# Root mean squares of a four-layer encoder on one core: the sum matmul spreads its result over all partitions, the root and reciprocal are taken on 256 columns, and fewer products are made ahead

## The chip, the core and the metric

The kernel runs on one core of a Trainium2 chip. The metric is device time in microseconds (us) of one execution of the whole program, in which all weights are read from HBM once. All data are float32. TensorE (PE in the profile) multiplies, VectorE (DVE) and ScalarE (ACT) work element by element, GpSimd (POOL) makes a few masks, and SyncE (SP) issues the loads of the weights.

## The reference

The input is 256 positions of 1024 features. Four layers each do a half-step feed-forward block, a mixer and another half-step feed-forward block; every block is normed before and after.

```python
def rms_norm(x, g):
    y = x * lax.rsqrt(jnp.mean(x * x, axis=-1, keepdims=True) + EPS)
    return y * g

def swiglu(h, w_in, w_out):
    gate, up = jnp.split(h @ w_in, 2, axis=-1)          # 1024 -> 2 x 2816
    return (jax.nn.silu(gate) * up) @ w_out             # 2816 -> 1024

for i in range(4):
    x = x + 0.5 * rms_norm(swiglu(rms_norm(x, g[0]), ff1_in[i], ff1_out[i]), g[1])
    h = rms_norm(x, g[2])
    m = mixer(i % 3)(h)         # 0: chunked attention, 1: gMLP, 2: differential attention
    x = x + rms_norm(m, g[3])
    x = x + 0.5 * rms_norm(swiglu(rms_norm(x, g[4]), ff2_in[i], ff2_out[i]), g[5])
```

So there are 12 blocks (8 feed-forward blocks, 4 mixers), 12 norms ahead of a block and 12 behind one. Each norm needs, for each of the 256 positions, one sum of squares over 1024 features, a root and a reciprocal.

## The kernel before

**Layout.** Features lie on the partitions, positions on the columns: the residual `xr` is 128 partitions x 8 tiles x 256 columns. A sum over features is therefore a sum over 8 tiles (done on DVE, tile by tile) and then over 128 partitions (done by a matmul).

**Products.** Each float32 factor is split into a high part (ACT, lines 127 and 315) and a low remainder (DVE, lines 130 and 330), both of a type that PE multiplies quickly; a product is made of three matmuls (high x high, low x high, high x low). Weights come in pieces of 128 x 1024 through three raw buffers; the class `Stream` splits them some pieces ahead of their use. The order of work on PE, DVE and ACT is the order in which the program writes it down.

**The end of a block.** `Branch.tile_done` (line 369) is called for each of the 8 output tiles: ACT squares the tile (line 376) and scales it by the gain (line 377), DVE adds the square to a running sum (line 387). At the last tile the sum over partitions is taken in two steps, once for the running sum and once for the last square: `column_sums` (line 237) uses the squares as the stationary operand and one column of ones as the moving one, in two halves of 128 positions, so that the sums come out with positions on the partitions (128 x 2). `Branch.finish` (line 393) takes the root (ACT, line 247) and the reciprocal (DVE, line 249) of these 128 x 2 numbers. Then `spread2` turns them back into a row that stands on all partitions: two matmuls (line 254) with the column repeated 128 times as the stationary operand and the identity as the moving one. DVE reads this row from PSUM (`fb`).

**The start of the next block.** `Normed` works in the order of `PARTS`: tiles 6, 7, 4 and 5, 0 and 1, 2 and 3. For each part DVE multiplies the tile by `fb` (line 476) and adds it to the residual (line 482), ACT takes the high part (line 315), DVE the low part (line 330). The first products of the next block follow in the same order of tiles (`JOIN`): four column blocks of weights, lines 510 (narrow) or 694 (wide). The norm ahead of the block is applied only later, to the products: `sums` and `spread` of `Normed` make its row `bc` from the sum of squares in the same way (`column_sums`, root, reciprocal on 128 x 2, `spread2`), and ACT copies it to SBUF (line 345). The three attention blocks use both the 128 x 2 form (`tok`) and the row; the gMLP block sends `tok` through DRAM (`spread_later`).

**Products made ahead.** Between the last product of one block and the first of the next PE would have nothing to do. `Ahead` fills this with products of the next block for some feature tiles `ks`. Since the update is x + y·f with f not yet known, it makes the products of x and of y separately (into two PSUM tiles, `ps` and `share`) for the first of the four column blocks; `scale` multiplies the y part by f later (line 458 or 461 and 462) and `join` adds the two (line 466). In `project_pair` and `Wide.block` the products that were made ahead are left out. There are two forms:

- narrow (weights stationary, 256 columns, line 451): from a mixer to the second feed-forward block (4 times, with `late=True`, where the y parts are made as `YLATE` says) and from a feed-forward block to the next layer (3 times). `ks` is (0, 1, 2, 3, 5): 5 tiles x 3 matmuls x 2 (x and y) = 30 matmuls ahead, 15 left out later.
- wide (activations stationary, 512 columns, line 449): from the first feed-forward block to the mixer, 4 times. `ks` is (1, 2, 3): 18 matmuls ahead, 9 left out later. Here only the first half of the positions is made ahead, and f is used as a 128 x 1 column (`update.f[:, 0:1]`, line 458).

The matmuls ahead are handed out in portions: 4 between the two sums (each wide one counts as two), 8 while the root is taken, the rest behind `spread2`. At the very end of the program there is no next block, and matmuls on a constant (`Warm`, line 233) stand in their places.

Of the kernel before, what the change touches and what calls it, by code (L numbers as in the profile page):

```python
# [9 lines left out]
F32 = mybir.dt.float32  # L10
BF16 = mybir.dt.bfloat16
F32R = mybir.dt.float32r
AF = mybir.ActivationFunctionType
# [3 lines left out]
P = 128  # L17
D = 1024
S = 256
# [28 lines left out]
ORDER = _order(range(KD))  # L48

PARTS = ((6, 7), (7, 8), (4, 6), (0, 2), (2, 4))  # L50
YLATE = {4: (0, 1, 2), 5: (3, 5)}
JOIN = _order([k for a, b in PARTS for k in range(a, b)])
DUMMY = [2, 1, 1] + [1, 0, 0] * 3 + [0] * 12

# [2 lines left out]
def encoder_trunk_kernel(  # L57
# [14 lines left out]
    nc = tc.nc  # L72

    const = ctx.enter_context(tc.tile_pool(name="const", bufs=1))
    wpool = ctx.enter_context(tc.tile_pool(name="wpool", bufs=3))
    act = ctx.enter_context(tc.tile_pool(name="act", bufs=1))
    tmp = ctx.enter_context(tc.tile_pool(name="tmp", bufs=2))
# [9 lines left out]
    class Stream:  # L87


        def __init__(self):  # L90
            self.pieces = {}
            self.raws = []
            self.now = 0
            self.split_next = 0
            self.allowed = SLOTS
            self.held = True
            self.pending = None
# [89 lines left out]
    def bank():  # L187
        return pst.tile([P, 512], F32, tag="pst", name="pst_t")
# [24 lines left out]
    nc.scalar.preload_act_table(AF.Sqrt)  # L213
    ident = const.tile([P, P], F32, name="ident")
    make_identity(nc, ident)
    ones = const.tile([P, 2], F32, name="ones")
    nc.vector.memset(ones, 1.0)
    eps_t = const.tile([P, 1], F32, name="eps_t")
    nc.vector.memset(eps_t, EPS)
    eps2_t = const.tile([P, 1], F32, name="eps2_t")  # L220
# [13 lines left out]

    Warm()(WARM)

    def column_sums(ps, sq, first, last):
        for h in range(2):
            nc.tensor.matmul(  # L239
                ps[:, h:h + 1], sq[:, h * P:(h + 1) * P], ones[:, 0:1],  # L240
                start=(first and h == 0), stop=(last and h == 1), skip_group_check=True,
            )

    def inv_sqrt(src, bias, n, scale):

        sd = small.tile([P, n], F32, tag=f"sd{n}", name="sd")
        nc.scalar.activation(sd, src, AF.Sqrt, bias=bias, scale=scale)
        r = small.tile([P, n], F32, tag=f"rs{n}", name="rs")
        nc.vector.reciprocal(r, sd)
        return r  # L250

    def spread(col, ps):

        nc.tensor.matmul(ps, col.broadcast_to([P, P]), ident, start=True, stop=True)  # L254

    def spread2(r):
        ps = bank()
        for h in range(2):
            spread(r[:, h:h + 1], ps[:, h * P:(h + 1) * P])
        return ps[:, 0:S]  # L260

    class Normed:

# [68 lines left out]
                    op0=ALU.mult, op1=ALU.subtract,  # L332
                )

        def sums(self, func):
            ps = bank()
            column_sums(ps, self.acc[:, 0, :], True, True)
            self.tok = inv_sqrt(ps[:, 0:2], eps_t, 2, 1.0 / D)
            nc.scalar.preload_act_table(func)

        def spread(self):

            ps = spread2(self.tok)
            self.bc = tmp.tile([P, S], F32, tag="rbc", name="rbc", bufs=1)
            nc.scalar.copy(self.bc, ps)

        def spread_later(self):

# [5 lines left out]
    class Branch:  # L354
# [15 lines left out]
        def tile_done(self, d, ps):  # L370
            if d == 0:
                self.acc = tmp.tile([P, S], F32, tag="ysq", name="ysq", bufs=1)
                if not self.yg:
                    self.yg = act.tile([P, KD, S], F32, tag="yg", name="yg")
            sq = tmp.tile([P, S], F32, tag="sq1", name="sq1") if d > 0 else self.acc
            nc.scalar.activation(sq, ps, AF.Square)
            nc.scalar.activation(self.yg[:, d, :], ps, AF.Copy, scale=self.gain[:, d:d + 1])
            if d == KD - 1:
                self.ss = bank()
                column_sums(self.ss, self.acc, True, False)  # L380
                self.fill = self.ahead or Warm()
                if self.ahead:
                    self.ahead.begin()
                self.fill(4)
                column_sums(self.ss, sq, False, True)
            elif d > 0:
                nc.vector.tensor_tensor(self.acc, self.acc, sq, op=ALU.add)
            elif self.n:
                nc.vector.scalar_tensor_tensor(self.acc, self.n.acc[:, 0, :], EPS, sq, op0=ALU.mult, op1=ALU.add)
            if self.ahead:  # L390
                self.ahead.tile_done(d, self.yg)

        def finish(self):

            f = inv_sqrt(self.ss[:, 0:2], eps2_t if self.n else eps_t, 2, 1.0 / D)
            self.fill(8)
            fb = spread2(f)
            self.fill(36 if self.ahead else 12)
            return Update(self.yg, f, fb, self.ahead)

    class Ahead:


        def __init__(self, gain, wide=False, late=False):
            self.gain, self.wide, self.late = gain, wide, late
            self.ks = (1, 2, 3) if wide else (0, 1, 2, 3, 5)
            self.x, self.y, self.todo = {}, {}, []

        def parts(self, dst, src, scale):
# [44 lines left out]
        def scale(self, update):  # L454

            if self.wide:
                self.fy = tmp.tile([P, 512], F32, tag="hf", bufs=3, name="fy")
                nc.scalar.activation(self.fy, self.share, AF.Copy, scale=update.f[:, 0:1])
            else:
                self.fy = tmp.tile([P, S], F32, tag="gs", name="fy")  # L460
                nc.scalar.copy(self.fy, self.share[:, 0:S])
                nc.vector.tensor_tensor(self.fy, self.fy, update.fb, op=ALU.mult)
# [5 lines left out]
    class Update:  # L468


        def __init__(self, yg, f, fb, ahead):
            self.yg, self.f, self.fb, self.ahead, self.t = yg, f, fb, ahead, {}

        def multiply(self, a, b):
            t = tmp.tile([P, 2, S], F32, tag="upd", name="upd")[:, 0:b - a, :]
# [75 lines left out]
    def ffn(l, which, update, ahead):  # L551
        n = Normed(update, g_sb[:, l, 4 * which, :])
# [6 lines left out]
        first = l == 0 and which == 0  # L559
# [21 lines left out]
        def between(jp):  # L581
            def at(i):
                if i < 3:
                    step()
                if jp == 1 and i == 0:
                    n.sums(AF.Silu)
                if jp == 1 and i == 1:
                    n.spread()
                if jp == 1 and i == 2:
                    gate(0, held[:, :, 0:S], held[:, :, S:2 * S])  # L590
                    step()
            return at
# [176 lines left out]
    def attention(n, softmax, transposes, v_done, mix, prepare=lambda: None, soon=lambda: None):  # L769

        wide = Wide(n)
# [3 lines left out]

        def early(j):
            if j == 0:
                n.sums(AF.Exp)
                v_done(0, ps_v)
            if j == 1:  # L780
                n.spread()
            if j == 2:
                prepare()

# [20 lines left out]
        last = KD // 2 - 1  # L805
# [118 lines left out]
    def mixer_b(l, i, update):  # L924
        n = Normed(update, g_sb[:, l, 2, :])
        ahead = Ahead(g_sb[:, l, 4, :], late=True)
# [19 lines left out]
        wide = Wide(n)  # L946
# [4 lines left out]

        def between(q):
            if q == 0:
                n.sums(AF.Gelu)
                n.spread_later()
            if q == 1:
                v_done(0, ps_v)
# [5 lines left out]
        r = inv_sqrt(mv[:, :, 1], eps_t, 2, 1.0)  # L963
# [34 lines left out]
        for jp in range(KD // 2):  # L998
            ps = pair()
# [266 lines left out]
```

## Time and profile before

| what | value |
|---|---|
| median of 3 runs | 1955.42 us (1954.46 to 1955.93) |
| the profiled execution, its own time | 1959.09 us |
| its span in the profile | 1957.4 us, 1.7 us less than its own time |
| PE busy | 1941.6 us, 12,435 matmul records |
| DVE, ACT busy | 1385.1 us, 1177.5 us |
| weights and other reads from HBM | 347.44 MB, 178 GB/s over the span |

How to read it: a row of the timeline gives the start, the length, the engine, the source line, the operation with what it writes and reads, and how many neighbours of one line are merged (x4). PEld is the load of the stationary operand; it runs ahead of its matmul by about 0.1 to 0.2 us, and since each matmul here has its own load, the distance between starts of loads is what one matmul really takes of PE. The length of a PE row contains its latency, and rows overlap. A float32 matmul that is not split shows as two loads and two matmuls (x4 stands for two matmuls). A number in brackets is idle time of the engine just before, with what ended it.

### The profile page before, as it was taken

To read this page: it belongs to the slowest core of one execution; us is meant where nothing else is said; L and a number is where in the kernel's file an instruction comes from. 1 tells how busy PE (TensorE), PEld (TensorE's weight loads), DVE (VectorE), ACT (ScalarE), POOL (GpSimd) and SP (SyncE) were. 2 spreads that over 40 slices of the span, in tenths; PEclk is the share of its full clock that TensorE was granted. 3 is DMA by queue.
4 is the path that set the end of the run, shared out by engine and by line. 5 is a ranking of instruction groups with operands and counts; after the bars stand their busy time and mean duration, and the time that the engine had idled before them with its cause. 6 is when DMAs were issued, how large, how long until landed. Compare 5 with 4: busy or idle time off the path is not lost.

```text
span 1957.4 us, 30171 instructions
## 1 busy us (share of the span) xinstructions
PE 1941.6 (99%) x12435; PEld 1750.1 (89%) x12435; DVE 1385.1 (71%) x1905; ACT 1177.5 (60%) x1826; POOL 6.7 (0%) x21
## 2 busy tenths in 40 slices
PE   9999999999999999999999999999999999999998
PEld 8888999888988888888988899988898889999887
DVE  6775767866777667867676668786667666868763
ACT  6655657656555555756565655675656565666652
POOL 0000000000000000000000000000000000000000
PEclk9999999999999999999999999999999999999999
DMA  7555534654455553554455535255546454535551
GB/s 260 201 187 200 188 108 153 233 188 180 173 194 188 199 158 147 207 196 177 159 207 190 198 145 181 109 196 194 191 151 214 176 204 159 197 125 182 200 201 44
DMA packets 50473, 350.43 MB, mean 179 GB/s; under 512 B 5760, under 2 KB 6016, under 8 KB 9120
## 3 DMA queue, kind: packets, MB, share of 16 engines
q1 hardware_dynamic: 48096, 341.86, 48.9%
q10 hardware_dynamic: 2160, 6.52, 0.9%
q8 instruction: 97, 1.59, 0.3%
q0 software_dynamic: 80, 0.13, 0.0%
q14 instruction: 40, 0.33, 0.0%
HBM read 347.44 MB, written 1.05 MB: 178 GB/s over the span
## 4 chain that ended last, share of the span: by engine, by line
PE 97%; DVE 1%; DMA 1%; ACT 0%; issue 0%; ACTq 0%; SPq 0%; DVEq 0%
PE pp_t L177 45%; PE pp_t L179 23%; PE pp_t L529 8%; PE pp_t L169 6%; PE pp_t L510 3%; PE pp_t L694 3%; PE pp_t L653 2%; DMA w_raw<-in_w 1%; PE pp_t L734 1%; PE pp_t L451 1%; PE pst_t L766 1%; PE pst_t L451 1%; PE pst_t L239 1%; PE pst_t L254 1%; PE pp_t L449 0%; PE pp_t L888 0%
## 5 line engine op out<-in xcount | busy, mean ns | idle before, releaser
L130 DVE TENSOR_TENSOR w_lo<-w_raw,w_hi 128x1024 fp32r<-128x1024 f32 (+1 forms) x649 | 774.7, 1217 | 57.9 <-ACT w_hi L127 57.8
L127 ACT CAST w_hi<-w_raw 128x1024 fp32r<-128x1024 f32 (+1 forms) x649 | 667.6, 1046 | 122.4 <-PE pp_t L177 84.1
L177 PE MATMUL pp_t<-xp,w_hi 128*128 128x512 f32 x2560 | 642.5, 393 | 0.0
L177 PEld LDWEIGHTS pp_t<-xp,w_hi 128*128 128x128 f32 x2560 | 460.2, 189 | 82.4
L179 PEld LDWEIGHTS pp_t<-xp,w_lo 128*128 128x128 f32 x2560 | 349.2, 190 | 25.1
L179 PE MATMUL pp_t<-xp,w_lo 128*128 128x256 f32 x2560 | 356.8, 282 | 0.0
L600 DVE TENSOR_TENSOR gu<-pp_t,share 128x512 f32<-128x512 f32 x160 | 110.6, 691 | 209.4 <-ACT share L599 209.3
L599 ACT COPY share<-pp_t 128x512 f32<-128x512 f32 x160 | 93.5, 585 | 179.3 <-PE pp_t L179 179.3
L177 PE MATMUL pp_t<-h,w_hi 128*128 128x512 f32 x672 | 175.7, 393 | 0.0
L177 PE MATMUL pp_t<-l,w_hi 128*128 128x512 f32 x560 | 148.8, 394 | 0.0
L570 ACT ACTIVATE gs<-gs 128x512 f32<-128x512 f32 x88 | 55.7, 632 | 141.0 <-DVE gs L569 141.0
L177 PEld LDWEIGHTS pp_t<-h,w_hi 128*128 128x128 f32 x672 | 117.7, 189 | 17.9
L529 PE MATMUL pp_t<-xp,w_hi 128*128 128x256 f32 x832 | 124.3, 288 | 1.7 <-ACT xp L315 1.4
L177 PEld LDWEIGHTS pp_t<-l,w_hi 128*128 128x128 f32 x560 | 100.0, 189 | 20.1 <-DVE l L579 2.9
L529 PEld LDWEIGHTS pp_t<-xp,w_hi 128*128 128x128 f32 x832 | 111.5, 193 | 4.2 <-ACT xp L315 1.6
L179 PEld LDWEIGHTS pp_t<-h,w_lo 128*128 128x128 f32 x672 | 97.7, 190 | 10.3
L367 DVE TENSOR_TENSOR yg<-pp_t,share 128x256 f32<-128x256 f32 x56 | 23.8, 424 | 110.3 <-ACT share L366 110.3
L179 PE MATMUL pp_t<-h,w_lo 128*128 128x256 f32 x672 | 100.6, 282 | 0.0
L179 PEld LDWEIGHTS pp_t<-l,w_lo 128*128 128x128 f32 x560 | 79.6, 190 | 6.1
L179 PE MATMUL pp_t<-l,w_lo 128*128 128x256 f32 x560 | 84.8, 282 | 0.0
L315 ACT ACTIVATE xp<-xr,g_sb 128x256 fp32r<-128x256 f32 x96 | 44.8, 503 | 58.6 <-DVE xr L482 56.5
L529 PE MATMUL pp_t<-xp,w_lo 128*128 128x256 f32 x416 | 73.8, 284 | 0.0
(198 smaller groups left out, 2297.3 us busy)
## 6 DMA issues: line engine op xcount, KB each, us to landing
w_raw<-in_w SPq DMA_DIRECT2D x322, 1024.0 KB, 4.8
l<-in_a_bias ACTq DMA_DIRECT2D x8, 512.0 KB, 8.8
w_raw<-in_w SPq DMA_DIRECT2D x3, 512.0 KB, 8.8
out_y<-xr SPq DMA_DIRECT2D x4, 256.0 KB, 2.1
xr<-in_x_t SPq DMA_DIRECT2D x2, 384.0 KB, 7.0
w_raw<-in_w SPq DMA_DIRECT2D x2, 256.0 KB, 4.7
l<-in_b_ws ACTq DMA_DIRECT2D x1, 512.0 KB, 5.4
l<-in_b_ln_g ACTq DMA_DIRECT2D x1, 512.0 KB, 9.3
```

Source lines behind the costliest of these rows:

```text
L127: nc.scalar.copy(hi[:, cols], raw[:, cols])
L130: nc.vector.tensor_tensor(lo[:, cols], raw[:, cols], hi[:, cols].bitcast(F32), op=ALU.subtract)
L169: nc.tensor.matmul(o, w_[:, at + i, :], x(k)[:, low, :], start=(start and i == 0 and m == 0), stop=(stop and k == ks[-1] and m == 2),)
L177: nc.tensor.matmul(o, wh[:, at + i, :], x(k), start=(start and i == 0), stop=False, skip_group_check=True)
L179: nc.tensor.matmul(o[:, 0:S], wl[:, at + i, :], x(k)[:, 0, :], start=False, stop=(stop and k == ks[-1]), skip_group_check=True,)
L315: nc.scalar.activation(self.h[:, k, :], xr[:, k, :], AF.Copy, scale=gain[:, k:k + 1])
L510: nc.tensor.matmul(o, part[:, k, :], n.x[:, k, int(low), :], start=((k, low) == JOIN[0] and i == 2 and part is ws[i][0]), stop=((k, low) = ...
L529: nc.tensor.matmul(o, part[:, k, :], n.x[:, k, low, :], start=(at == 0), stop=(at == 3 * KD - 1))
L570: nc.scalar.activation(gs, gs, AF.Silu)
L599: nc.scalar.copy(share, ps[:, :, S:2 * S])
L600: nc.vector.tensor_tensor(at.t[:, e], ps[:, :, 0:S], share, op=ALU.add)
L694: nc.tensor.matmul(self.ps[:, t, :], xs[:, kk, t * P:(t + 1) * P], ws, start=((kk, low) == self.order[0] and ws is wh and not (t == 0 and ...
```

## The change

The sums over partitions are made with 128 x 128 ones as the stationary operand and the squares as the moving one: one matmul of 256 columns gives the row of sums on all 128 partitions at once. Root (ACT) and reciprocal (DVE) are taken on 128 x 256 instead of 128 x 2, in SBUF, and `spread2` goes, behind a block (`finish`) and ahead of one (`Normed.spread`; in the feed-forward blocks `sums` goes too). The row of `finish` and the row of `Normed` share one buffer (`rbc`). Where a 128 x 2 or 128 x 1 form is still needed, it is made besides: `Normed.sums` in the mixers as before, and for the wide transition one more matmul of one column next to each of the two sums, whose root and reciprocal are taken in `Ahead.scale`. `ks` shrinks from 5 to 4 tiles (narrow) and from 3 to 2 (wide), and the portions change: 2 matmuls between the two sums where the transition is narrow and none where it is wide, all others behind the second sum. The stand-in matmuls at the end of the program go.

```diff
-YLATE = {4: (0, 1, 2), 5: (3, 5)}
+YLATE = {4: (0, 1), 5: (2, 3)}
...
-    def column_sums(ps, sq, first, last):
-        for h in range(2):
-            nc.tensor.matmul(
-                ps[:, h:h + 1], sq[:, h * P:(h + 1) * P], ones[:, 0:1],
-                start=(first and h == 0), stop=(last and h == 1), skip_group_check=True,
-            )
+    def column_sum(ps, sq, h, start, stop):
+        nc.tensor.matmul(ps, sq[:, h * P:(h + 1) * P], ones, start=start, stop=stop, skip_group_check=True)
+    def column_sums(ps, sq, start, stop):
+        nc.tensor.matmul(ps, ones.broadcast_to([P, P]), sq, start=start, stop=stop, skip_group_check=True)
...
+    def inv_sqrt_row(src, bias):
+        r = tmp.tile([P, S], F32, tag="rbc", name="row", bufs=1)
+        nc.scalar.activation(r, src, AF.Sqrt, bias=bias, scale=1.0 / D)
+        nc.vector.reciprocal(r, r)
+        return r
...
         def spread(self):
-            ps = spread2(self.tok)
-            self.bc = tmp.tile([P, S], F32, tag="rbc", name="rbc", bufs=1)
-            nc.scalar.copy(self.bc, ps)
+            ps = bank()[:, 0:S]
+            column_sums(ps, self.acc[:, 0, :], True, True)
+            self.bc = inv_sqrt_row(ps, eps_t)
...
                 self.ss = bank()
-                column_sums(self.ss, self.acc, True, False)
-                self.fill = self.ahead or Warm()
-                if self.ahead:
-                    self.ahead.begin()
-                self.fill(4)
-                column_sums(self.ss, sq, False, True)
+                wide = self.ahead and self.ahead.wide
+                for sq_, first in ((self.acc, True), (sq, False)):
+                    column_sums(self.ss[:, 0:S], sq_, first, not first)
+                    if wide:
+                        column_sum(self.ss[:, S:S + 1], sq_, 0, False, not first)
+                    if self.ahead and first:
+                        self.ahead.begin()
+                        if not wide:
+                            self.ahead(2)
...
         def finish(self):
-            f = inv_sqrt(self.ss[:, 0:2], eps2_t if self.n else eps_t, 2, 1.0 / D)
-            self.fill(8)
-            fb = spread2(f)
-            self.fill(36 if self.ahead else 12)
-            return Update(self.yg, f, fb, self.ahead)
+            eps = eps2_t if self.n else eps_t
+            fb = inv_sqrt_row(self.ss[:, 0:S], eps)
+            if self.ahead:
+                self.ahead(36)
+            return Update(self.yg, self.ss, eps, fb, self.ahead)
...
-            self.ks = (1, 2, 3) if wide else (0, 1, 2, 3, 5)
+            self.ks = (2, 3) if wide else (0, 1, 2, 3)
...
-                nc.scalar.activation(self.fy, self.share, AF.Copy, scale=update.f[:, 0:1])
+                f = inv_sqrt(update.ss[:, S:S + 1], update.eps, 1, 1.0 / D)
+                nc.scalar.activation(self.fy, self.share, AF.Copy, scale=f)
...
                 if jp == 1 and i == 0:
-                    n.sums(AF.Silu)
-                if jp == 1 and i == 1:
                     n.spread()
+                    nc.scalar.preload_act_table(AF.Silu)
```

In the attention blocks `sums` and `spread` now both come behind the first column block (before, `spread` came behind the second), and the load of the next function table of ACT, which `sums` issued, follows them; in the gMLP block `sums` and `spread_later` stay, with that load between them.

More of the change, by code (lines that the diff above doesn't have):

```diff
@@ L215, in encoder_trunk_kernel @@
     make_identity(nc, ident)
-    ones = const.tile([P, 2], F32, name="ones")
+    ones = const.tile([P, 1], F32, name="ones")
     nc.vector.memset(ones, 1.0)
@@ L250, in inv_sqrt @@
         return r
[L252 to L260, printed above, removed]
+    def inv_sqrt_row(src, bias):
[3 more added lines that the diff above has]
+        return r
     class Normed:
@@ L333, in low, with sums, spread @@
                 )
-        def sums(self, func):
+        def sums(self):
             ps = bank()
-            column_sums(ps, self.acc[:, 0, :], True, True)
-            self.tok = inv_sqrt(ps[:, 0:2], eps_t, 2, 1.0 / D)
-            nc.scalar.preload_act_table(func)
-        def spread(self):
-            ps = spread2(self.tok)
-            self.bc = tmp.tile([P, S], F32, tag="rbc", name="rbc", bufs=1)
-            nc.scalar.copy(self.bc, ps)
+            for h in range(2):
+                column_sum(ps[:, h:h + 1], self.acc[:, 0, :], h, h == 0, h == 1)
+            self.tok = inv_sqrt(ps[:, 0:2], eps_t, 2, 1.0 / D)
+        def spread(self):
+            ps = bank()[:, 0:S]
+            column_sums(ps, self.acc[:, 0, :], True, True)
+            self.bc = inv_sqrt_row(ps, eps_t)
         def spread_later(self):
@@ L468, in encoder_trunk_kernel, with __init__ @@
     class Update:
-        def __init__(self, yg, f, fb, ahead):
-            self.yg, self.f, self.fb, self.ahead, self.t = yg, f, fb, ahead, {}
+        def __init__(self, yg, ss, eps, fb, ahead):
+            self.yg, self.ss, self.eps, self.fb, self.ahead, self.t = yg, ss, eps, fb, ahead, {}
         def multiply(self, a, b):
@@ L777, in early @@
             if j == 0:
-                n.sums(AF.Exp)
+                n.sums()
                 v_done(0, ps_v)
-            if j == 1:
                 n.spread()
+                nc.scalar.preload_act_table(AF.Exp)
             if j == 2:
@@ L953, in between @@
             if q == 0:
-                n.sums(AF.Gelu)
+                n.sums()
+                nc.scalar.preload_act_table(AF.Gelu)
                 n.spread_later()
```

## The prediction

> **What bounds the kernel now.** I read the page first: busy shares, then the chain that ended last.
>
> ```profile
> span 1957.4 us, 30171 instructions
> ...
> PE 1941.6 (99%) x12435; PEld 1750.1 (89%) x12435; DVE 1385.1 (71%) x1905; ACT 1177.5 (60%) x1826; POOL 6.7 (0%) x21
> ...
> PE 97%; DVE 1%; DMA 1%; ACT 0%; issue 0%; ACTq 0%; SPq 0%; DVEq 0%
> ```
>
> PE carries 97% of the chain, so a matmul that goes is time that goes, unless PE then waits for something that it did not wait for. That can happen at the 11 passages from block to block. So I read the timeline of one narrow passage (mixer to feed-forward block, first layer) row by row.
>
> ```profile
> 310.92 0.54 PEld L239 LDWEIGHTS pst_t<-ones,ysq 128*128 128x128 f32 x4
> ...
> 311.24 0.38 ACT L376 ACTIVATE sq<-pp_t 128x256 f32<-128x256 f32 x1 [1.19 <-PE pp_t L169]
> ...
> 311.85 0.53 PEld L239 LDWEIGHTS pst_t<-ones,sq 128*128 128x128 f32 x4
> ...
> 312.50 0.26 ACT L247 ACTIVATE sd<-pst_t,eps_t 128x2 f32<-128x2 f32 x1 [0.51 <-PE pst_t L239]
> ...
> 312.80 0.17 DVE L249 RECIPROCAL rs<-sd 128x2 f32<-128x2 f32 x1 [1.24 <-ACT sd L247]
> ...
> 313.69 0.19 PEld L451 LDWEIGHTS pp_t<-ahead,w_hi 128*128 128x128 f32 x1
> ...
> 314.00 0.42 DVE L476 TENSOR_TENSOR upd<-yg,pst_t 128x256 f32<-128x256 f32 x1 [1.04 <-PE pst_t L254]
> ...
> 314.91 0.51 ACT L315 ACTIVATE xp<-xr,g_sb 128x256 fp32r<-128x256 f32 x1 [2.15 <-DVE xr L482]
> ...
> 315.83 0.19 PEld L510 LDWEIGHTS pp_t<-xp,w_hi 128*128 128x128 f32 x1
> ...
> 316.91 0.87 DVE L330 SCALAR_TENSOR_TENSOR xp<-xr,g_sb,xp 128x256 fp32r<-128x256 f32 x2
> ```
>
> Two threads run from the last product at 310.92. PE: sums, 30 products ahead, broadcast, and the first product of the next block at 315.83. Beside it ACT and DVE: square, root, reciprocal, update, high part of tile 6, ready at 314.91 + 0.51 = 315.42. PE comes 0.41 us after it: PE is the later thread, with little to spare. The wide passage (first layer) has more, 202.13 against 200.72 + 0.51 = 201.23, so 0.90:
>
> ```profile
> 196.74 0.54 PEld L239 LDWEIGHTS pst_t<-ones,ysq 128*128 128x128 f32 x4
> ...
> 197.06 0.38 ACT L376 ACTIVATE sq<-pp_t 128x256 f32<-128x256 f32 x1 [1.95 <-PE pp_t L169]
> ...
> 199.49 0.19 PEld L449 LDWEIGHTS pp_t<-w_hi,ahead 128*128 128x128 f32 x1
> ...
> 199.80 0.42 DVE L476 TENSOR_TENSOR upd<-yg,pst_t 128x256 f32<-128x256 f32 x1 [1.03 <-PE pst_t L254]
> ...
> 200.72 0.51 ACT L315 ACTIVATE xp<-xr,g_sb 128x256 fp32r<-128x256 f32 x1 [2.15 <-DVE xr L482]
> ...
> 202.13 0.41 PEld L694 LDWEIGHTS pp_t<-w_hi,xp 128*128 128x128 f32 x2
> ...
> 202.71 0.87 DVE L330 SCALAR_TENSOR_TENSOR xp<-xr,g_sb,xp 128x256 fp32r<-128x256 f32 x2
> ...
> 211.34 0.67 ACT L458 ACTIVATE fy<-pst_t,rs 128x512 f32<-128x512 f32 x1
> ...
> 212.39 0.42 DVE L297 TENSOR_TENSOR sqacc<-sqacc 128x256 f32<-128x256 f32 x1
> ```
>
> **Prices on PE.** From starts of loads: 18 narrow products from 313.69 to 315.83 are 0.119 us each; 12 wide ones from 199.49 to 202.13 are 0.22 each. The unsplit float32 matmuls are priced in the norm inside a feed-forward block, where they stand between full streams:
>
> ```profile
> 328.35 0.54 PEld L239 LDWEIGHTS pst_t<-ones,sqacc 128*128 128x128 f32 x4
> 328.80 1.69 PEld L177 LDWEIGHTS pp_t<-xp,w_hi 128*128 128x128 f32 x8
> ...
> 331.59 0.53 PEld L254 LDWEIGHTS pst_t<-ident,rs 128*128 128x128 f32 x4
> 332.04 1.69 PEld L177 LDWEIGHTS pp_t<-xp,w_hi 128*128 128x128 f32 x8
> ```
>
> The pair of sums takes 0.45 us (to 328.80), the broadcast pair of line 254 takes 0.45 (to 332.04). Each is four passes of 0.11. The new sum is one matmul, two passes of 256 columns, which before does not show. Below it costs two passes, 0.22, if columns are free; above, twice that, 0.45, if a pass grows with its columns. I take 0.45: the split products do grow, 0.119 to 0.22, when the columns double.
>
> Then the account of PE is short. The broadcast pair goes 23 times (12 behind a block, 8 ahead of a feed-forward block, 3 in attention): -10.35. Each new sum replaces a pair of sums at 0.45 for 0.45. Attention keeps its pair and gets a sum besides: 3 x 0.45 = +1.35. A wide passage gets two matmuls of one column, 0.22 each: 4 x 0.44 = +1.8. Six products ahead go and three come back in the next block, so three net: narrow 7 x 3 x 0.119 = -2.5, wide 4 x 3 x 0.22 = -2.6. Together -12.3 us of PE work.
>
> **What of it reaches the end.** The new row needs a root and a reciprocal on 256 columns:
>
> ```profile
> L599 ACT COPY share<-pp_t 128x512 f32<-128x512 f32 x160 | 93.5, 585 | 179.3 <-PE pp_t L179 179.3
> ...
> L345 ACT COPY rbc<-pst_t 128x256 f32<-128x256 f32 x11 | 4.1, 375 | 0.0
> ```
>
> ```profile
> L387 DVE TENSOR_TENSOR ysq<-ysq,sq 128x256 f32<-128x256 f32 x72 | 30.6, 424 | 32.6 <-ACT sq L376 32.5
> ...
> L867 DVE TENSOR_SCALAR ex<-ex,rsum 128x256 f32<-128x256 f32 x32 | 11.1, 348 | 0.0
> ...
> L746 DVE TENSOR_SCALAR nm<-nm 128x4 f32<-128x4 f32 x8 | 1.4, 170 | 0.3
> ```
>
> ```profile
> L759 DVE RECIPROCAL rsum<-sums x16: 166/168/172, 232.4 to 1728.9; 128x4 f32<-128x4 f32 x16
> ```
>
> ```profile
> L1077 DVE RECIPROCAL rl<-sums x8: 155/156/158, 1188.0 to 1239.0; 128x2 f32<-128x2 f32 x8
> ```
>
> Root: ACT grows by (585 - 375) / 256 = 0.82 ns a column, so 0.26 + 0.21 = 0.47 us. Reciprocal: no row has it on more than 4 columns. Below, 0.35, as line 867 on 256 columns; as an ordinary one-pass operation, 0.42, as line 387; above, by its own growth from 2 to 4 columns, (168 - 156) / 2 = 6 ns a column, 0.156 + 254 x 0.006 = 1.68, and by the extremes, (172 - 155) / 2 = 8.5 ns, 2.3. I take 0.42, because growth over so few columns is no rate: on 4 columns the reciprocal (168) costs what line 746 does (170), and that kind of operation needs only 348 on 256, 0.7 ns a column.
>
> The Trainium skill speaks against this value: its page "VectorE: DVE Perf Modes", section "First, the fixed hardware budget", has the reciprocal as an iterative divide with a repeat count of 8. Read as eight clocks a column at the page's 0.96 GHz, an estimate is 2.1 us above the fixed part, and the sum would be slower by some 10 us. No run here shows it.
>
> Narrow passage, from 310.92: sum to 311.37, two products to 311.61; the square is done at 311.24 + 0.38 = 311.62 and seen at about 311.68. PE: second sum to 312.13, 22 products to 314.75. That is 1.08 before 315.83; three products more behind it cost 0.36. Other thread: the root began 0.65 after the second sum's load (311.85 to 312.50); I allow 0.70 for the longer passes, so 312.38, done 312.85; reciprocal 312.89 to 313.31 (0.04 from engine to engine, as 312.76 to 312.80); update at 313.35 instead of 314.00, since the way through PE is gone. High part of tile 6 ready at 315.42 - 0.65 = 314.77, against PE at 314.75: the cover is just used up. The low part of tile 6 (first half of line 330's pair, 317.35, now 316.70) is needed 16 products on, 316.66. Both are even, so I allow 0.12 of waiting: -0.6 each, 7 times, -4.2.
>
> Wide passage, from 196.74: sum and column 0.67, the square seen at 197.50, another 0.67, 12 products of 0.22: 200.81 instead of 202.13, and 0.66 back in the next block. Update: 197.50 + 0.70 + 0.47 + 0.04 + 0.42 + 0.04 = 199.17, 0.63 earlier; tile 6 ready at 200.60, under PE's 200.81. The low part, 203.15 - 0.63 = 202.52, is needed 8 products on, 202.57. So -0.6 each, for layers 0, 2 and 3: -1.8.
>
> The wide passage adds a wait: line 458 needs a reciprocal that stands on DVE behind line 297. It starts at 212.39 + 0.42 - 0.63 + 0.25 = 212.43, not 211.34. ACT stands for 1.1 us; behind it are the mixer's own loads, issued by ACT, and the casts of weights (line 127). PE is covered there by pieces split ahead. Nothing on SP or POOL is passed. The second sum's bank of an attention block waits for line 458, done 213.10, before PE wants it at about 213.3.
>
> In the gMLP block that cover is missing, as the chain shows:
>
> ```profile
> 712.05 13.68 DMA w_raw<-in_w
> 740.44 4.55 PE pp_t L169 x24
> 745.89 2.87 PE pp_t L169 x24
> ```
>
> There a load of weights of 13.68 us ends last, so the 0.6 of PE is swallowed; the chain ahead of the load runs through ACT and DVE, so it moves between -0.63 (earlier update) and +1.1 (the new wait). I take 0. Behind the wait 24 products took 4.55 where the same 24 then took 2.87; this slow spell may shift by up to 1.7 either way.
>
> Ahead of a feed-forward block PE does not wait at all: 8 x 0.45 = -3.6; the longer reciprocal on DVE (+0.25) and the gone copy on ACT are hidden by the blocks of products behind. Attention's +1.35 stands against the three broadcast pairs gone there: 0.
>
> ```profile
> 1946.54 0.38 ACT L376 ACTIVATE sq<-pp_t 128x256 f32<-128x256 f32 x1 [6.09 <-PE pp_t L169]
> ...
> 1949.02 1.28 DVE L476 TENSOR_TENSOR upd<-yg,pst_t 128x512 f32<-128x512 f32 x2 [0.88 <-PE pst_t L254]
> ```
>
> At the very end nothing covers the chain: 1946.98 + 0.70 + 0.47 + 0.04 + 0.42 + 0.04 = 1948.65, not 1949.02: -0.4.
>
> Sum: -4.2 - 1.8 + 0 - 3.6 + 0 - 0.4 = -10.0 us, of -12.3 of PE work. The profiled execution took 1959.09 us (span 1957.4 and 1.7 around it); 1949.1 is 0.51% less. On the median of 1955.42 that is **1945.5 us**.
>
> **The rivals.** First, the reciprocal pays by the column, 6 to 8.5 ns, so 1.68 to 2.3 us. It is on the path wherever the cover ends. At 1.68 it is 1.26 longer than I took: narrow, tile 6 ready at 316.03, so PE starts 0.2 later than before and has 0.36 more behind it, 7 x 0.56 = +3.9; wide, 201.86, 0.27 earlier but 0.66 more, 3 x 0.4 = +1.2; gMLP block about +1.1; end +0.9; feed-forward norms -3.6: +3.5. Each further 0.1 us counts 12 times, 1.2 us: at 2.3 it is +11. Middle +7, **1962 us**; it decides from about 1.3 us on. For it speaks the growth of 10 to 17 ns over two columns; against it line 746, which has the same cost on 4 columns and no such rate.
>
> Second, the gain of the passages is swallowed: PE arrives even with the other thread by my own count, and 0.5 us more anywhere in it (a root that waits for the column sum too, a slower matmul) takes most of the 6.0 there. Left are -3.6 and -0.4: **1951.5 us**. For it speaks that the margins are all under 0.1 in the narrow form; against it that each price has a near row.
>
> That the change does not do what it says I see no room for: no stage falls back on the old way.
>
> **How the numbers follow.** Forecast 0.60, slow reciprocal 0.30, swallowed 0.10. What a measurement of this kernel can tell from no change is about 0.2%, 3.9 us. Forecast and half of the swallowed case are faster, about 0.63 with a little taken off for the unknown; the slow reciprocal at its low end (+3.5) and the other half of the swallowed case lie within: 0.13; the rest of the slow reciprocal is slower: 0.24. The forecast's own range is 1942.5 (all 12.3 of PE arrive and the slow spell shrinks) to 1949 (waits of 0.3 in each passage). The range reaches up to the middle of the slow reciprocal, 1962.5; its upper half is left out.
>
> **What would show it.** Right: RECIPROCAL on 128x256 near 0.42 us; first product of the next block about 3.8 us after the first sum (before, 4.91) without a wait; the update's first multiply about 0.65 us earlier; no line 254; PE busy about 12 us less. Wrong: a reciprocal over 1.3 us, and PE waiting for line 315 at each passage; or a sum matmul over 0.5 us.

## The result and the profile after

| what | before | after |
|---|---|---|
| median | 1956.64 us (1954.46 to 1958.79, 6 runs) | 1971.86 us (1969.44 to 1973.36, 6 runs) |
| ratio after / before | | 1.0075, 95% interval 1.0065 to 1.0085 |
| the profiled execution, its own time | 1959.09 us | 1969.44 us |

The changed kernel is 0.75% slower, about 15 us; the forecast was 10 us faster. Its page:

```profile
span 1967.7 us, 29749 instructions
...
PE 1931.5 (98%) x12244; PEld 1735.0 (88%) x12244; DVE 1411.6 (72%) x1890; ACT 1171.6 (60%) x1800; POOL 7.0 (0%) x21
...
PE 91%; DVE 5%; ACT 2%; issue 1%; DMA 1%; ACTq 0%; SPq 0%; DVEq 0%
```

PE has 10.1 us less to do (1941.6 to 1931.5), and the span is 10.3 us longer. So PE now waits for some 20 us that it did not wait before; the chain says for whom: DVE and ACT carry 7% of it instead of 1%. The view of waits (who waited, for what, total, times, longest) gives the places:

```profile
PE pp_t L513 <- ACT xp L313: 8.3, 7, 1.2
PE pp_t L736 <- DVE qk L726: 4.5, 3, 1.6
PE pp_t L696 <- ACT xp L313: 3.8, 4, 0.9
```

Together they are 16.6 us. None of the three rows had a counterpart before: the 7 narrow passages, the 4 wide ones, and, away from every passage, the scores of the three attention blocks. The groups by form name the new work:

```profile
L257 DVE RECIPROCAL row<-row 128x256 f32<-128x256 f32 x23 | 40.3, 1753 | 41.1 <-ACT row L256 41.1
```

```profile
L256 ACT ACTIVATE row<-pst_t,eps_t 128x256 f32<-128x256 f32 x23 | 10.9, 474 | 18.5 <-PE pst_t L243 16.4 <-PE pst_t L239 2.2
...
L461 ACT ACTIVATE fy<-pst_t,rs 128x512 f32<-128x512 f32 x4 | 2.7, 687 | 5.6 <-DVE rs L250 5.6
```

The root is the 0.47 us that was forecast. The reciprocal takes 1.753 us, not 0.42. The last row shows that ACT stands 5.6 / 4 = 1.4 us ahead of line 461. The narrow passage whose rows were read before now looks so:

```profile
311.12 0.31 PEld L243 LDWEIGHTS pst_t<-ysq,ones 128*128 128x128 f32 x2
...
311.87 0.30 PEld L243 LDWEIGHTS pst_t<-sq,ones 128*128 128x128 f32 x2
...
312.61 0.47 ACT L256 ACTIVATE row<-pst_t,eps_t 128x256 f32<-128x256 f32 x1 [0.43 <-PE pst_t L243]
...
313.12 1.75 DVE L257 RECIPROCAL row<-row 128x256 f32<-128x256 f32 x1 [1.44 <-ACT row L256]
...
314.80 0.19 PEld L453 LDWEIGHTS pst_t<-ahead,w_hi 128*128 128x128 f32 x1
...
314.90 0.42 DVE L479 TENSOR_TENSOR upd<-yg,row 128x256 f32<-128x256 f32 x1
...
315.82 0.51 ACT L313 ACTIVATE xp<-xr,g_sb 128x256 fp32r<-128x256 f32 x1 [2.74 <-DVE xr L485]
...
316.38 0.19 PEld L513 LDWEIGHTS pp_t<-xp,w_hi 128*128 128x128 f32 x1 [1.38 <-ACT xp L313]
```

PE's last product ahead begins at 314.80; then PE is idle until the high part of tile 6 is there (315.82 + 0.51 = 316.33). Before, PE was the later thread; now it is ACT and DVE, and 1.75 us of their thread is the reciprocal. Cut at two points of every block, the first load of the sums at its end and the first product of the next block, the two traces compare like this (starts of PE's loads; lengths in us; means where a row counts several):

| stage | before | after | sum of the difference |
|---|---|---|---|
| start to the first sum | 196.74 | 194.70 | -2.0 |
| 7 narrow passages | 4.91 | 5.26 | +2.4 |
| 4 wide passages | 5.39 | 5.37 | 0.0 |
| 3 attention blocks | 108.31 | 110.63 | +7.0 |
| gMLP block | 78.88 | 81.52 | +2.6 |
| 7 feed-forward blocks | 184.25 | 184.16 | -0.6 |
| end | 11.14 | 12.15 | +1.0 |

The sum is the difference of the spans, +10.3. The first row has little to do with the change. From 9.8 to 13.2 us the granted clock was 0.50 before and 1.00 after, and the runs below need 195.9 to 196.3 us with such a stretch and 194.5 to 194.9 without it. Without this row +12.4 remain. The surprise stands in the fourth row.

### The profile page after: what moved, and what is told of

The parts are those of the page before. It is cut to its first block, busy times and chain, and to the rows that moved or that the text cites. A ratio compares the mean times of both kernels' runs of the same rounds, so it can differ in the third digit from the quotient of the medians.

```text
span 1967.7 us, 29749 instructions
## 1 busy us (share of the span) xinstructions
PE 1931.5 (98%) x12244; PEld 1735.0 (88%) x12244; DVE 1411.6 (72%) x1890; ACT 1171.6 (60%) x1800; POOL 7.0 (0%) x21
## 3 DMA queue, kind: packets, MB, share of 16 engines
q8 instruction: 96, 1.57, 0.3%
## 4 chain that ended last, share of the span: by engine, by line
PE 91%; DVE 5%; ACT 2%; issue 1%; DMA 1%; ACTq 0%; SPq 0%; DVEq 0%
PE pp_t L177 44%; PE pp_t L179 23%; PE pp_t L169 6%; PE pp_t L532 6%; PE pp_t L513 4%; PE pp_t L655 2%; PE pp_t L696 2%; DVE row L257 1%; DVE w_lo L130 1%; PE pp_t L736 1%; PE pst_t L243 1%; DVE xr L485 1%; DVE upd L479 1%; PE pst_t L768 1%; DMA w_raw<-in_w 1%
## 5 line engine op out<-in xcount | busy, mean ns | idle before, releaser
L179 PE MATMUL pp_t<-xp,w_lo 128*128 128x256 f32 x2560 | 356.9, 282 | 0.0
L532 PE MATMUL pp_t<-xp,w_hi 128*128 128x256 f32 x832 | 123.0, 287 | 1.9 <-ACT xp L313 1.0
L179 PEld LDWEIGHTS pp_t<-h,w_lo 128*128 128x128 f32 x672 | 97.7, 190 | 10.3
L513 PE MATMUL pp_t<-xp,w_hi 128*128 128x256 f32 x392 | 72.8, 286 | 8.3 <-ACT xp L313 8.3
```

The lines of the kernel that those rows point to most:

```text
L179: nc.tensor.matmul(o[:, 0:S], wl[:, at + i, :], x(k)[:, 0, :], start=False, stop=(stop and k == ks[-1]), skip_group_check=True,)
L513: nc.tensor.matmul(o, part[:, k, :], n.x[:, k, int(low), :], start=((k, low) == JOIN[0] and i == 2 and part is ws[i][0]), stop=((k, low) = ...
L532: nc.tensor.matmul(o, part[:, k, :], n.x[:, k, low, :], start=(at == 0), stop=(at == 3 * KD - 1))
```

## The experiments

The theory to start with: the reciprocal pays by the column, the passages and the end pay for it, and the attention blocks pay too, because the same 1.75 us stands on DVE ahead of the weights' remainders (line 130) there. The rival: the attention blocks pay for ACT, which stands for the factor of line 461.

**sizes**: the kernel before, with reciprocals and multiplications of 1 to 512 columns appended behind its last work on DVE.

```diff
+    for n in (1, 2, 4, 8, 16, 32, 64, 128, 256, 512):
+        nc.vector.reciprocal(scratch[:, 0:n], scratch[:, 0:n])
+        nc.vector.tensor_scalar_mul(scratch[:, 0:n], scratch[:, 0:n], 1.0)
```

> The kernel before, with ten reciprocals and ten plain multiplications by 1 appended after the outputs are sent, on 1, 2, 4, 8, ... 512 columns of a scratch tile. Theory (pays by the column): about 6.2 ns a column from the smallest size on, 0.55 us at 64, 0.95 at 128, 1.75 at 256, 3.35 at 512; the multiplication under 0.5 us at 512. Rival (a fixed price above some size): a step between two sizes and little growth after it.

The timeline of DVE at its end:

```profile
1954.06 0.18 DVE L1194 RECIPROCAL scratch<-scratch 128x4 f32<-128x4 f32 x1
...
1956.02 0.55 DVE L1194 RECIPROCAL scratch<-scratch 128x64 f32<-128x64 f32 x1
1956.61 0.20 DVE L1195 TENSOR_SCALAR scratch<-scratch 128x64 f32<-128x64 f32 x1
...
1958.09 1.75 DVE L1194 RECIPROCAL scratch<-scratch 128x256 f32<-128x256 f32 x1
1959.88 0.29 DVE L1195 TENSOR_SCALAR scratch<-scratch 128x256 f32<-128x256 f32 x1
1960.20 3.35 DVE L1194 RECIPROCAL scratch<-scratch 128x512 f32<-128x512 f32 x1
```

From 64 to 512 columns (3.35 - 0.55) / 448 = 6.25 ns a column, and the same rate holds at the low end: 0.15 + 4 x 0.00625 = 0.175 for 4 columns. The multiplication costs 0.20 us on 64 and 0.29 on 256 columns, 0.5 ns each. So the reciprocal costs some twelve times as much by the column as this multiplication.

**row_copy, row_copy_behind, row_copy_ahead**: the changed kernel with the reciprocal on 256 columns replaced by a multiplication by 0.1, everywhere, only behind the blocks (`finish`), or only ahead of them (`Normed.spread`). The norms lack their reciprocal there; everything else is as it was.

```diff
-        nc.vector.reciprocal(r, r)
+        nc.vector.tensor_scalar_mul(r, r, 0.1)
```

> Leaves out both reciprocals on 256 columns: the row is the root times 0.1, in one plain DVE operation of about 0.35 us with the same neighbours. All else is the changed kernel. Theory (the reciprocal's 1.75 us sets every new wait): the waits of PE for the high part of tile 6 go (7 x 1.46, 4 x 1.33, and 4 x 0.25 for its low part), the wait of the scores in attention goes (3 x 1.5), the end gains 1.4: about 22 us less than the changed kernel, so some 1949, or 0.4% under the kernel before. Rival (the 1.4 us for which ACT stands at the wide passage causes the wait of the scores): that 4.5 stays, 17 less. Rival (fewer products ahead leave PE idle whatever the row costs): PE still waits over 0.7 at each narrow passage, about 10 less.

> Leaves out the reciprocal on 256 columns behind the blocks alone (root times 0.1 instead); ahead of the blocks it stays. Theory: the passages and the end gain as with both left out, about 18 us less than the changed kernel, some 1954; the scores in attention still wait about 1.5 us, three times. If the wait of the scores came from the passages instead, it would go too and this would equal the kernel with both left out.

> Leaves out the reciprocal on 256 columns ahead of the blocks alone (feed-forward and attention; root times 0.1 instead); behind the blocks it stays. Theory: the feed-forward blocks do not move, since the reciprocal is hidden there; the wait of the scores in attention goes, 3 x 1.4: about 4 us less than the changed kernel, some 1967.5. Rival (ACT standing at the wide passage): no change.

| kernel | ratio to before | narrow | wide | attention | end |
|---|---|---|---|---|---|
| after | 1.0075 (1.0065 to 1.0085) | 5.26 | 5.37 | 110.63 | 12.15 |
| row_copy | 0.9972 (0.9961 to 0.9983) | 3.80 | 4.05 | 110.31 | 10.68 |
| row_copy_behind | 0.9976 (0.9966 to 0.9986) | 3.80 | 4.05 | 110.47 | 10.69 |
| row_copy_ahead | 1.0059 (1.0044 to 1.0074) | 5.26 | 5.37 | 110.32 | 12.14 |

```profile
L257 DVE TENSOR_SCALAR row<-row 128x256 f32<-128x256 f32 x23 | 6.8, 295 | 41.1 <-ACT row L256 41.1
```

The reciprocal behind the blocks is worth 1.46 us at each narrow passage and at the end, and 1.32 at each wide one, where the cheaper operation (the row above, from row_copy) is 1.753 - 0.295 = 1.46 us shorter: it stands on the path nearly whole. Ahead of the blocks it costs little: the feed-forward blocks keep their 184.17 us. But the attention blocks keep theirs too. The scores' wait, in row_copy:

```profile
PE pp_t L736 <- DVE qk L726: 3.7, 3, 1.5
```

It was 4.5. So the first theory fails there: the reciprocal accounts for 0.8 of the 4.5, and something else for the rest. The ratio of row_copy_ahead, about 3 us under that of the changed kernel, comes near the 4 us that were expected, but the two intervals overlap, and the wait that was to go is still 3.6 us there.

**f_early and spread_second**: two causes were left. Either ACT stands too long for the factor of line 461; f_early takes root and reciprocal of the 128 x 1 column in `finish`, behind those of the row. Or the row and the load of the Exp table, now behind the first column block of attention, hold up the casts of weights; spread_second puts them behind the second block again.

```diff
             fb = inv_sqrt_row(self.ss[:, 0:S], eps)
+            if self.ahead and self.ahead.wide:
+                self.ahead.f = inv_sqrt(self.ss[:, S:S + 1], eps, 1, 1.0 / D)
...
-                f = inv_sqrt(update.ss[:, S:S + 1], update.eps, 1, 1.0 / D)
-                nc.scalar.activation(self.fy, self.share, AF.Copy, scale=f)
+                nc.scalar.activation(self.fy, self.share, AF.Copy, scale=self.f)
```

> The changed kernel, but the root and reciprocal of the 128 x 1 column that scales the share of y are taken in finish, right behind those of the row, so line 461 does not wait on DVE. Theory (the scores' wait of 1.8 us in each attention block comes from ACT standing 1.4 us for this column, which delays the casts of weights and, behind their remainders on DVE, the q x k factor): the wait before the scores falls from 1.5 towards 0.3 in each of the three attention blocks, the gMLP block loses about 1 us too, and the time comes out 4 to 5 us under the changed kernel, ratio to the kernel before about 1.005. Rival (the wait comes from the spread and the table load having moved ahead of the second column block): the scores' wait stays at 1.5, the time within 1.5 us of the changed kernel, ratio about 1.007.

> The changed kernel, but in the attention blocks the row of the norm (sum matmul, root, reciprocal on 256 columns) and the load of the Exp table that follows it stand behind the second column block again, as in the kernel before. Rival theory (their move to the first column block delays the casts of weights on ACT by the table load and the root): the scores' wait of 1.5 us goes, each attention block is 1 to 1.5 us shorter, time 3 to 4.5 us under the changed kernel, ratio about 1.0055. Theory (ACT standing for the 128 x 1 column is the cause): scores' wait stays within 0.3 us, time as the changed kernel, 1.0075.

f_early came out at 1.0029 (1.0017 to 1.0041), by the ratios 9 us under the changed kernel where 4 to 5 were expected: each attention block is 1.2 to 1.6 us shorter (mean 109.18), and in its waits there is no row for the scores any more. spread_second came out at 1.0057 (1.0041 to 1.0072), attention 110.42, and its waits still say:

```profile
PE pp_t L736 <- DVE qk L726: 3.9, 3, 1.4
```

The ratio of spread_second is the one that its rival theory named (1.0055), but not for the rival's reason: the attention blocks are 0.2 us shorter, not 1 to 1.5, and the span of the profiled run is 1.0 us shorter in all; where the rest of the 3.5 us by the ratios comes from is not shown. f_early takes the scores' wait away and spread_second leaves most of it, so the wait comes in the main from the stand of ACT.

The gMLP block pays for it too. It has no scores; there PE waits until ACT, behind its casts, has read the products of line 945 (946 in f_early) out of PSUM. The changed kernel and f_early:

```profile
PE pp_t L169 <- ACT l L945: 2.1, 1, 2.1
```

```profile
PE pp_t L169 <- ACT l L946: 1.4, 1, 1.4
```

The block takes 80.5 to 83.2 us, and this wait 2.1 to 4.3, in all six kernels that take the factor only where it is used (the changed kernel, the three row_copy kernels, spread_second, ks_back). It takes 76.4 to 79.2 us, with at most 1.4 of this wait, in the three that take it in `finish` (f_early and, further down, copy_f_early and act_rsqrt). The two groups do not overlap; their means are 81.6 and 78.1. Within a group the length moves by 3 us, so one pair of runs does not give the size. By which steps the stand gets there is not shown: ACT's cast ahead of line 945 waits for a load of weights, which lies between the two.

How 1.4 us on ACT, 15 us ahead of the scores, reach PE is seen in the timeline of the first attention block. The changed kernel, from the factor's root to the factor of the scores:

```profile
210.17 0.24 ACT L248 ACTIVATE sd<-pst_t,eps_t 128x1 f32<-128x1 f32 x1
...
211.23 0.42 DVE L295 TENSOR_TENSOR sqacc<-sqacc 128x256 f32<-128x256 f32 x1
...
211.57 0.15 DVE L250 RECIPROCAL rs<-sd 128x1 f32<-128x1 f32 x1
...
211.82 0.69 ACT L461 ACTIVATE fy<-pst_t,rs 128x512 f32<-128x512 f32 x1 [1.40 <-DVE rs L250]
211.84 2.11 ACTq L850 DMA_DIRECT2D l<-in_a_bias  x4
214.05 2.00 ACT L127 CAST w_hi<-w_raw 128x1024 fp32r<-128x1024 f32 x2 [1.54 <-PE pst_t L243]
...
219.79 5.69 DVE L130 TENSOR_TENSOR w_lo<-w_raw,w_hi 128x1024 fp32r<-128x1024 f32 x5
225.41 1.21 DVE L726 TENSOR_TENSOR qk<-pp_t,row 128x1024 f32<-128x1024 f32 x1
...
226.74 1.45 PEld L736 LDWEIGHTS pp_t<-qk 64*128 64x128 f32 x24 [1.61 <-issue]
```

And f_early:

```profile
210.98 0.82 ACTq L851 DMA_DIRECT2D l<-in_a_bias  x2
211.51 0.67 ACT L462 ACTIVATE fy<-pst_t,rs 128x512 f32<-128x512 f32 x1
211.83 1.11 ACTq L851 DMA_DIRECT2D l<-in_a_bias  x2
213.04 1.99 ACT L127 CAST w_hi<-w_raw 128x1024 fp32r<-128x1024 f32 x2 [0.86 <-issue]
...
218.78 5.70 DVE L130 TENSOR_TENSOR w_lo<-w_raw,w_hi 128x1024 fp32r<-128x1024 f32 x5
224.40 1.22 DVE L727 TENSOR_TENSOR qk<-pp_t,row 128x1024 f32<-128x1024 f32 x1
```

The first product of the block is at 200.08 in the changed kernel and at 201.41 in f_early; counted from there, the casts begin at 13.97 and 11.63. The 2.3 us are the stand and what queued behind it: the issues of four loads of the bias (2.11 us on ACT's queue), which in f_early begin beside earlier ACT work and in the changed kernel start only at line 461. Behind the casts DVE has five remainders of weights in a row, and behind those the factor of the scores, at 25.33 and 22.99. No engine catches up on the way, and PE reaches the scores before the factor does. (The changed kernel's row puts the idle time ahead of the casts down to the sum of line 243. In spread_second that sum comes later, and the casts still begin 0.1 us behind the last issue, at 214.09, as they do in the two kernels above.)

**ks_back**: the changed kernel with as many products ahead as before, to ask whether the thinner cover is to blame for the passages.

```diff
-YLATE = {4: (0, 1), 5: (2, 3)}
+YLATE = {4: (0, 1, 2), 5: (3, 5)}
...
-            self.ks = (2, 3) if wide else (0, 1, 2, 3)
+            self.ks = (1, 2, 3) if wide else (0, 1, 2, 3, 5)
```

> The changed kernel, but as many products made ahead as in the kernel before (5 tiles narrow, 3 wide, the same order of y parts). Theory (the reciprocal of 1.75 us sets when the first product of the next block can start; the fewer products ahead have only made PE wait for it longer): the passages stay at 5.26 and 5.38 us, since the products ahead still end before the high part of tile 6, the products given back behind each passage go (0.36 x 7 and 0.66 x 4, 5.1 us), and the time is about 5 us under the changed kernel, ratio 1.005, still slower than before. Rival (the cover was too thin: with all products ahead again PE waits no longer and the old length is back): narrow passages 4.9, time 7 to 8 us under the changed kernel, ratio 1.0035. A third possibility, that PE becomes the later thread again: narrow passages longer than 5.26, gain under 3 us.

The passages stayed as expected (narrow 5.26, wide 5.41), and the feed-forward blocks got their 0.36 us back (183.81). But the ratio is 1.0067 (1.0054 to 1.0081), not 1.005: the attention blocks grew to a mean of 112.15. PE has fewer products left there, so it comes to the scores still earlier, and its wait (4.6 for two of them, 2.0 for one) grew past 2 us. Then something new shows. In two windows of the first attention block, the wait and the 24 products of the scores behind it, the columns are length, busy times of the five engines, PEclk, share and rate of the DMA:

```profile
226.00:228.60 2.60, 0.19 (x2) 0.00 (x0) 2.52 (x3) 0.80 (x1) 0.00 (x0) 0.91 1.02 416
228.60:231.50 2.90, 2.84 (x24) 2.67 (x24) 2.31 (x4) 1.20 (x2) 0.00 (x0) 0.50 1.00 373
```

After the wait the granted clock is 0.50, and the 24 products take 2.9 us instead of the 1.57 of the changed kernel.

**copy_f_early**: both causes out at once (row_copy and f_early together; the norms lack their reciprocal on 256 columns), to see whether anything is left unexplained.

> Both causes taken away at once: the changed kernel with the reciprocals on 256 columns replaced by a plain multiplication by 0.1 (which leaves the reciprocal out of the norms) and with the 128 x 1 column taken in finish. Theory (these two are all that the forecast had wrong): the scores' wait goes as in f_early (about 1.5 x 3, and 1 to 2 us in the gMLP block), the passages stay at the 3.80 and 4.05 us of row_copy, and the time comes out 5 to 7 us under row_copy, ratio to the kernel before about 0.994, the 0.9949 of the forecast or a little under. Rival (something else costs time in the mixers too): ratio 0.996 or above, with a wait of PE in the mixers that the kernel before does not have.

The ratio is 0.9937 (0.9924 to 0.9951). Passages 3.80 and 4.05, attention 109.10, gMLP block 78.65, end 10.68, and no wait at passages or scores. The rival, a further cost in the mixers, finds nothing there.

**row_ffn_only**: the kernel before, with only the norm ahead of the feed-forward blocks made the new way.

```diff
+        def row(self, func):
+            ps = bank()[:, 0:S]
+            sum_row(ps, self.acc[:, 0, :])
+            self.bc = tmp.tile([P, S], F32, tag="rbc", name="rbc", bufs=1)
+            nc.scalar.activation(self.bc, ps, AF.Sqrt, bias=eps_t, scale=1.0 / D)
+            nc.vector.reciprocal(self.bc, self.bc)
+            nc.scalar.preload_act_table(func)
...
-                    n.sums(AF.Silu)
-                if jp == 1 and i == 1:
-                    n.spread()
+                    n.row(AF.Silu)
```

> The kernel before, with only the norm ahead of the feed-forward blocks changed: one sum matmul on all partitions, root and reciprocal on 256 columns, no broadcast pair. Ends of blocks, mixers and products ahead are those of the kernel before. Theory (the reciprocal's 1.75 us costs nothing where products cover it, and the broadcast pair was on PE's path): no wait of PE appears, each of the 8 feed-forward blocks is 0.45 us shorter, 3.6 us in all, ratio 0.998, range 0.9970 to 0.9990. Rival (a DVE that is held for 1.75 us in one piece delays the remainders of the weights and gives the gain back): 1.000 or above, with a wait of PE for line 130's remainders or for the products' partner behind the norm.

0.9980 (0.9971 to 0.9989), 1954.22 us, every feed-forward block 0.48 us shorter (183.77); the passages, the attention blocks and the end keep their lengths. (The gMLP block went from 78.88 to 77.20 us, but it is 78.27 in sizes, which does not touch it.) The timeline of the same norm as in the prediction's rows:

```profile
327.74 0.30 PEld L264 LDWEIGHTS pst_t<-sqacc,ones 128*128 128x128 f32 x2
328.07 1.79 PEld L177 LDWEIGHTS pp_t<-xp,w_hi 128*128 128x128 f32 x8
...
328.99 1.75 DVE L357 RECIPROCAL rbc<-rbc 128x256 f32<-128x256 f32 x1 [0.58 <-ACT rbc L356]
```

The sum is paid with 0.33 us to the next load and 0.10 in the eight products behind it (1.79, before 1.69), and the reciprocal of 1.75 us is covered by products that need it only later.

**act_rsqrt**: f_early with root and reciprocal taken by one function of ACT, so that DVE has no reciprocal in any norm.

```diff
-        nc.scalar.activation(r, src, AF.Sqrt, bias=bias, scale=1.0 / D)
-        nc.vector.reciprocal(r, r)
+        nc.scalar.activation(r, src, AF.Abs_reciprocal_sqrt, bias=bias, scale=1.0 / D)
```

> f_early with root and reciprocal taken as one function of ACT (Abs_reciprocal_sqrt), for the rows and for the 128 x 1 and 128 x 2 columns, and its table loaded where that of the root was. Theory: nothing stands on DVE between the sums and the update, so the passages are as short as with the plain multiplication or 0.3 us shorter where PE is not the later thread (narrow 3.5 to 3.8, wide 4.05), the end loses 1.75 us, and the ratio to the kernel before is 0.993 to 0.995. Rival (the function costs ACT much more on 256 columns than the root's 0.47 us, or its table is loaded once more at each passage, 1.28 us each): passages of 5 us, ratio 1.00 or above.

1941.62 us, ratio 0.9920 (0.9906 to 0.9934): it beats both kernels, by a little more than the 0.993 to 0.995 that were expected. Its narrow passage:

```profile
308.25 0.30 PEld L243 LDWEIGHTS pst_t<-ysq,ones 128*128 128x128 f32 x2
...
309.73 0.48 ACT L254 ACTIVATE row<-pst_t,eps_t 128x256 f32<-128x256 f32 x1 [0.42 <-PE pst_t L243]
310.24 0.42 DVE L477 TENSOR_TENSOR upd<-yg,row 128x256 f32<-128x256 f32 x1 [1.45 <-ACT row L254]
...
311.16 0.51 ACT L310 ACTIVATE xp<-xr,g_sb 128x256 fp32r<-128x256 f32 x1 [0.95 <-DVE xr L483]
...
312.04 0.19 PEld L511 LDWEIGHTS pp_t<-xp,w_hi 128*128 128x128 f32 x1
```

The function costs what the root costs (0.48), the update starts 0.03 us behind it, and PE, at 312.04, is the later thread again, 0.37 us behind the high part (311.16 + 0.51). The passage is 3.79 us long.

## Why the prediction was wrong

**The step that failed** is the price of the reciprocal: "I take 0.42, because growth over so few columns is no rate." The growth was the rate: 6 ns a column from rows of 2 and 4 columns, 6.25 measured to 512. The comparison with line 746 misled, since at 4 columns a fixed 0.15 us hides any rate: 4 x 6.25 = 25 ns there, against 2 ns for an ordinary operation. The estimate from the Trainium skill ("VectorE: DVE Perf Modes", "First, the fixed hardware budget"), eight clocks a column, was nearer, with a price by the column a third too high: 6.25 ns at the page's 0.96 GHz are 6 clocks.

**The size of the rival.** The first rival had the true mechanism, and at 1.753 us its sum is about +4.4; the stages say +12.4. Its terms, in order. Narrow: tile 6 ready 5.18 us behind the first sum by its working, 5.21 measured; with the products given back about 0.63 a passage, measured 0.7. Wide: PE's first product came 0.19 later than worked out; 0.14 of it is tile 6 (5.33 us behind the first sum, 5.19 by the working), because the root also waits for the column's sum (the 2.2 us of line 239 in the row of line 256, 0.54 each). With the products given back in the mixer that makes 0.65 instead of 0.46 each. End: 0.97 against 1.01. What is missing is the other failed sentence, "PE is covered there by pieces split ahead", of the wait that the change adds at line 461. The stand of ACT was near the forecast (1.4 against 1.1 us), its cover was not there: 1.2 to 1.6 us in each attention block. I had named what queues behind it, loads and casts, but had followed them no further than ACT, where the next two steps (five remainders on DVE, then the factor of the scores) lead to PE. Of the 8 us between +4.4 and +12.4 the attention blocks' part that f_early takes away is 4.4. The gMLP block, which the forecast put at 0 and the rival at +1.1, came out at +2.6 in the one pair of profiled runs; by the two groups above the late factor is worth some 3.5 there. The forecast had allowed for up to 1.1 of wait and 1.7 of a slow spell, but not added them.

**What held.** PE's busy time fell by 10.1 us where 12.3 of work were worked out; it also holds the latency of the last product before each new wait, and in copy_f_early, which lacks these waits, it fell by 14.8, so the 12.3 are borne out only roughly. The root: 0.47 and 0.474. The sum matmul, 0.45: 0.33 + 0.10. The norms ahead of the feed-forward blocks, -3.6 in all: in row_ffn_only 8 x 0.48 = 3.8 by its stages, 0.2% by its ratio. PE's own thread: narrow 3.83 worked out, 3.80 measured where nothing else is late; wide 4.07 and 4.05. And the sum: the forecast's ratio was 1945.5 / 1955.42 = 0.9949 with a reciprocal of 0.42 us and no wait at the scores; copy_f_early, which has 0.295 in its place and no such wait, is at 0.9937. 0.125 us less at 12 places are 1.5 us or 0.0008, so the same account gives 0.9941. The two failed steps are what lies between the -10 of the forecast and the measured +15. Undone one at a time, with the ratios: the reciprocal, against a multiplication of 0.295 us, 1.0075 - 0.9972 = 1.0%, 20 us; the stand of ACT 1.0075 - 1.0029 = 0.5%, 9 us, of which the stages of one pair of profiled runs show 6.7 (4.4 in the attention blocks, 2.35 in the gMLP block; with 3.5 for the latter, from the two groups, it is 7.9).

## What to carry to other kernels

A growth of a few nanoseconds over two columns should be priced as a rate until a row with many columns says otherwise; when the whole sum hangs on one such operation, look for the form that does without it (here one function of ACT, 0.48 us for what cost 0.47 + 1.75). A longer operation is free only where products that do not need it stand behind it: the same 1.75 us cost nothing ahead of a feed-forward block and nearly all of itself behind every block. And follow an added wait through every queue behind it to the next instruction of the bounding engine, not just to the end of the first queue.

## What the runs showed of the hardware

The reciprocal on DVE: 0.15 us and 6.25 ns a column, from 1 to 512 columns. A float32 sum with 256 moving columns is two passes, and costs 0.43 us, as much as the pair of sums with one column each (0.45).

A wait of PE can cost more than itself. Over the runs above, the 24 products of the scores took 1.57 us where the loads before and behind the wait lay up to 1.94 us apart, and 2.32, 2.10 and 2.89 us in ks_back, where they lay 2.34, 2.44 and 2.84 apart, with a granted clock of 0.50 in the last. The Trainium skill ("TensorE: Matmul & The Clock Gate", "What's actually happening") has the clock halved after an idle window of about 3.4 us; among the scores here waits of 2.3 us were enough, and 1.94 were not. The length of a wait alone does not decide it: in the gMLP block of spread_second loads 3.35 us apart (727.52 and 730.87) were followed by 3.4 us at a granted clock of 1.00.
